# A hybrid recurrent diffusion step on one core: a new order for the last gates, splits and sums of the mixing stage

## The chip, the core and the metric

The kernel runs on one core of a Trainium2 chip. A core has TensorE (PE, matrix products into PSUM), VectorE (DVE), ScalarE (ACT, functions through tables), GpSimd (POOL) and SyncE (SP, whose queue here issues most loads). Each engine runs its own instructions in the order in which the program issues them, and waits at semaphores for the others. The metric is the device time of one execution in microseconds (us); a kernel is run several times and the median is told.

## The reference, cut to what matters

One layer for 640 tokens (128 of a prompt, 512 of a sample; 1024 features). The part around the change:

```python
hn = _rmsnorm(x, g_pre_mix) * (1 + sc1) + sh1
xa, ga, xs = jnp.split(hn @ w_in, [D_LRU, 2 * D_LRU], axis=-1)
ua = _dwconv(xa, conv_w, conv_b)
# both directions d, per block of 64 channels:
r = sigmoid(ua @ w_r[d] + b_r[d]);  i = sigmoid(ua @ w_i[d] + b_i[d])
log_a = -LRU_C * r * softplus(-lam[d]);  a = exp(log_a)
b = sqrt(-expm1(2 * log_a)) * (i * ua)
h = linear_scan(a, b, h0[d])
ya = gelu(ga) * (h[0] + h[1])
ys = ...                      # the S5 branch, 512 features
gate_a, gate_b = jnp.split(sigmoid(hn @ w_gate + b_gate), 2, axis=-1)
m = (gate_a * (ya @ w_proj_lru) + gate_b * (ys @ w_proj_s5)) @ w_out
x = x + g1 * _rmsnorm(m, g_post_mix)
# then a SwiGLU feed-forward (w_ff_in, w_ff_out), also normed and modulated
```

## The kernel before, in words

**Tiling.** Features lie on the 128 partitions, the 640 tokens along the free dimension, so 1024 features are eight tiles ("channels tiles" 0 to 7) of 128 x 640. Every fp32 product is made of three products of reduced-precision halves: high x high, low x high and high x low (`mtile`, lines 175 to 185), each in two halves of 320 tokens. So each weight block and each activation is *split* once: ScalarE copies it to its high part (`wh`, `yah`, `mh`), and VectorE subtracts that to get the low part (`wl`, `yal`, `ml`).

**Weights.** All weight blocks ("units") are listed in the order of use (lines 198 to 245). `split_next` (line 133) takes the next one: it allocates `wh` and `wl` from pools of three buffers each, issues ScalarE's copy and VectorE's subtraction, and then lets SP's queue issue loads up to four units ahead (`fetch_to`, four `raw` buffers). So a split waits for a load, for a free `wh` (which the products of the third unit before it must release), and its low part stands in VectorE's queue at the place where `split_next` was called. `use` splits on demand. Some units (blocks of `w_mod`) are not split: `mod_step` (line 569) multiplies them as they are, eight matmuls of one modulation step, into a PSUM tile that is held from the first step to the last.

**Tiles.** PSUM holds four tiles of 128 x 1024 fp32 (`psq`, line 67); one product takes one of them until its result is evacuated. Token tiles come from a pool of 20 (`ttile`), those of the recurrent unit from a pool of 27 (`lru`, line 1274). A new tile waits until a buffer is free; ScalarE, VectorE or GpSimd stand still meanwhile.

**The order is written out by hand** (`manual_schedule`, line 48): each engine's queue is the order of the calls. Around the change (lines 1307 to 1476):

- The loop at line 1307 runs over pairs of channel tiles of the recurrent unit; in its last round it makes the inputs of tiles 6 and 7. Then follows the tail of that unit for tiles 4 to 7, interleaved with the S5 projection.
- `gate_job(15)` (line 845): product of the sixteenth gate (`gate_mm`), its bias and two sigmoids on ScalarE, and a store to DRAM issued from ScalarE's queue. `gate_load` and line 1395 load gates back on GpSimd's queue (tiles `gld`, `gts`).
- `lru_gates(c)` (line 1172): four products of six matmuls (`q_gl`: two directions, r and i), each with a sigmoid on ScalarE (`ri`).
- `lru_scan(c)` (line 1220): four scans on VectorE into two tiles `hh` and their sum; `lru_mul(c)`: times the GELU branch; `lru_split(c)`: the two halves `yah`, `yal`; `lru_iu(c)`: i times u, two products on VectorE.
- `lru_decay` (line 1192): for two tiles, four tanh into tiles `ta`, then four exponentials in place, then whatever is passed as `then`, then four square roots; with table loads on ScalarE between. `lru_drive` (line 1212): for each tile four VectorE instructions, each 128 x 644.
- `ps5(m)` (line 1363), m = 0 to 7: an S5 projection of 24 matmuls (`q_p`), evacuated by a product with a gate on VectorE (`gld`). The sum over both branches is later made in the same tile.
- `pl_first(m)`, m = 0 to 2 (line 1378): the "first low part" of the output projection, over the first six of eight channel tiles, 36 matmuls (`q_pl`), copied to `plp` by ScalarE.
- The loop at line 1442 goes over the items `a0 a1 a2 f3 b0 f4 f5 f6 f7` (line 227). Items a are the low parts above, items f are whole projections of 48 matmuls; item b makes the "second parts" for m = 0 to 2 (12 matmuls each), adds them to `plp` and multiplies with the gate on VectorE. `mix_add(m)` adds the S5 part on GpSimd, `mix_split(m)` makes the halves `mh`, `ml`. Each item but the first begins with a `split_next` and, up to the eighth, a modulation step.
- `wo_mm(i, mid)` (line 1507): a block of 128 tokens times `w_out` (`q_wo`), 48 matmuls of 512 columns. `wo_evac` and `hn2_tile` norm the result and transpose it for the feed-forward.

All small arithmetic goes through helpers, so rows carry their lines: L59 is `tt` (VectorE or GpSimd, two tensors), L62 is `act` (ScalarE), L65 is `mm`, L130 a weight load on SP's queue, L1217 and L1229 the drive and the scans.

Of the kernel before, what the change touches and what calls it, by code (L numbers as in the profile page):

```python
# [39 lines left out]
def hybrid_step_kernel(ctx: ExitStack, tc: tile.TileContext, A, y_prompt, y_sample, o_lru, o_re, o_im):  # L40
# [92 lines left out]
    def split_next(eng=None, lo_eng=None, late=None):  # L133

        while state["split"] < len(units):
            i = state["split"]
            u = units[i]
            state["split"] += 1
            if not u["split"]:
                continue  # L140
            fetch_to(i + 1)
            pool, bufs = u.get("pool", (wp, 3))
            u["hi"] = pool.tile(u["shape"], F32R, tag="wh", bufs=bufs, name="wh")
            u["lo"] = pool.tile(u["shape"], F32R, tag="wl", bufs=bufs, name="wl")
            if eng is None:
                act(u["hi"], u["raw"], AF.Copy)
            else:
                eng.tensor_copy(out=u["hi"], in_=u["raw"])
            if late is None:
                tt(u["lo"], u["raw"], u["hi"], ALU.subtract, lo_eng)  # L150
            else:
                late.append(lambda: tt(u["lo"], u["raw"], u["hi"], ALU.subtract))
            fetch_to(i + 5)
            return True
        return False
# [689 lines left out]
    def gate_job(m, pool=None, q=None):  # L845
        q = gate_mm(m) if q is None else q
        g = ttile("gate", pool=pool)
        seg_act(g, q, AF.Sigmoid, shift(q, vec("b_gate", GO[m])))
        if pool is None:
            ACT.dma_start(out=gd[GO[m]], in_=g[:, 0:T])  # L850
        return g[:, 0:T]
# [320 lines left out]
    def lru_gates(c):  # L1172
        u, uh, ul, wh, wl = fr[c]
        r = {}
        for d, i in DI:
            q = psq("q_gl")
            a = 2 * d + i
            for b, (ww, xx) in enumerate(((wh, uh), (wl, uh), (wh, ul))):
                for h in range(2):
                    mm(q[:, 190 + 322 * h:190 + 322 * (h + 1)], ww[:, a], xx[:, 322 * h:322 * (h + 1)],  # L1180
                       b == 0, b == 2)
            t = ttile("ri", pool=lp)[:, 0:644]
            act(t, q[:, 190:834], AF.Sigmoid, bias=vec(("lru_b_r", "lru_b_i")[i], d * 8 + c))
            r[d, i] = t
        bk[c] = r
# [166 lines left out]
        warm(AF.Sigmoid)  # L1352

    gate_t = {}
    gate_job(15)

    def gate_load(m):
        gate_t[m] = ttile("gld")[:, 0:T]
# [4 lines left out]
    def ps5(m):  # L1363
        q = psq("q_p5")
        mtile(q, wblocks(U_PS[m // 2], 4, (m % 2) * 128, ahead=0), ys, range(4))
        t = gate_t.pop(8 + m)
        tt(t, q[:, 192:832], t, ALU.mult)
        mp.append(t)
# [9 lines left out]
    def pl_first(m):  # L1378
        q = psq("q_pl")
        pl_mm(q, "a", m, range(KP))  # L1380
        act(plp[:, m], q[:, 192:832], AF.Copy)

    split_next()
    lru_gates(6)
    lru_gates(7)
    for m in range(8, 14):
        gate_load(m)
    lru_scan(4)
# [4 lines left out]
    gts = htile("gts", F32, KD * T).rearrange("p (m t) -> p m t", m=8)  # L1393
    for m in range(8):
        POOL.dma_start(out=gts[:, m], in_=gd[m])
    split_next()
    ps5(0)
    lru_iu(6)
    lru_iu(7)
    gate_load(14)  # L1400
    gate_load(15)
    ps5(1)
    ta = lru_decay((6, 7), None, lambda: [lru_split(4), lru_split(5)])
    ps5(2)
    split_next()
    ps5(3)
    lru_drive(ta, (6, 7))
    for c in (6, 7):
        act(gel[c], gel[c], AF.Gelu_apprx_tanh)
    ps5(4)  # L1410
    split_next()
    ps5(5)
    lru_scan(6)
    split_next()
    ps5(6)
    lru_scan(7)
    ps5(7)
    lru_mul(6)
    lru_mul(7)
    split_next()  # L1420
# [20 lines left out]
    pt = {}  # L1441
    for j, (part, m) in enumerate(items):
        if j:
            split_next()
            if j < 8:
                mod_step(2, j, mod_raw(2, j))
            if part == "a":
                pl_first(m)
            elif part == "b":
                for i in range(NP1):  # L1450
                    q = psq("q_pl")
                    pl_mm(q, "b", i, range(KP, KD))
                    tt(plp[:, i], q[:, 192:832], plp[:, i], ALU.add)
                    tt(plp[:, i], plp[:, i], gts[:, i], ALU.mult)
                    pt[i] = plp[:, i]
                    mix_add(i)
            else:
                q = psq("q_pl")
                pl_mm(q, "f", m, range(KD))
                pt[m] = gts[:, m] if m < 7 else ttile("t7")[:, 0:T]  # L1460
                tt(pt[m], q[:, 192:832], gts[:, m], ALU.mult)
                if m < 7:
                    mix_add(m)
                for i in {NP1 + 1: (NP1,), NP1 + 2: (0, 1), NP1 + 3: (2, 4), NP1 + 4: (5,)}.get(m, ()):
                    mix_split(i)
        if j == 2:
            q = psq("q_nl")
            transpose(q[0:16, 0:128], nl.rearrange("p d k -> p (d k)"))
            nlo = ttile("nlo", pool=lp)
            DVE.tensor_copy(out=nlo[0:16, 0:128], in_=q[0:16, 0:128])  # L1470
            SP.dma_start(out=o_lru[0, 0].rearrange("d (k p) -> (d k) p", p=128), in_=nlo[0:16, 0:128])
        if j == 3:
            pre2 = mod_pre(2)
    mix_split(6)
    fetch_to(state["split"] + 4)
    lpool.__exit__(None, None, None)

# [378 lines left out]
```

## Time and profile before

| | us |
|---|---|
| median of three runs | 1039.13 |
| the three runs | 1036.62, 1039.13, 1042.95 |
| the profiled execution | 1037.07 |
| its span, first to last instruction | 1035.3 |
| TensorE busy | 989.7 |
| VectorE, ScalarE, GpSimd busy | 668.3, 461.0, 197.2 |

The mean granted clock of TensorE over the span is 0.988 of full speed (1.00 is the level of 2.4 GHz, 0.50 that of 1.2 GHz). In a timeline each row is one instruction or a run of equal ones: start and length in us from the start of the span, engine and line, operation, output tile <- input tiles, shape, count; in brackets how long the engine stood idle just before it, and whose instruction released it. A wait for several things is put down to the one that came last. Neighbouring rows overlap a little where instructions are pipelined.

### The profile page before, as it was taken

What the parts mean: (1) busy time and instruction counts of PE and PEld (TensorE: products, weight loads), DVE (VectorE), ACT (ScalarE), POOL (GpSimd) and SP (SyncE); (2) the same over time, 40 slices, a digit from 0 to 9 for tenths busy, and PEclk for the clock granted to TensorE, in tenths of its full rate; (3) what the DMA queues carried; (4) which work ended last, traced back from release to release, by engine and by line L of the source; (5) the groups of instructions that cost most, each with busy time, mean ns of one, the idle gap of its engine ahead of it and who ended that gap; (6) DMA issues with size and microseconds to landing.
All of it is one profiled execution on the core that took longest, in us unless ns stands there. A gap on an engine that the chain in (4) does not pass through costs nothing.

```text
span 1035.3 us, 16728 instructions
## 1 busy us (share of the span) xinstructions
PE 989.7 (96%) x6649; PEld 911.1 (88%) x6649; DVE 668.3 (65%) x1103; ACT 461.0 (45%) x748; POOL 197.2 (19%) x200
## 2 busy tenths in 40 slices
PE   5999999979999999999999989999999999999997
PEld 3698988879999999987877889999999999888885
DVE  5789899962477989782575785555555565434113
ACT  5535423234349889732242443444454454333112
POOL 4000000000000000300310274555555551000002
PEclk9999999989999999999999999999999999999999
DMA  9944276543213221747562312223322223522202
GB/s 305 322 115 128 68 210 199 186 152 96 63 42 102 61 73 49 259 133 210 178 201 104 121 43 82 81 83 87 96 83 82 83 82 122 206 79 82 70 13 101
DMA packets 135901, 125.57 MB, mean 121 GB/s; under 512 B 17320, under 2 KB 115384, under 8 KB 135824
## 3 DMA queue, kind: packets, MB, share of 16 engines
q1 hardware_dynamic: 129888, 111.82, 35.1%
q10 hardware_dynamic: 4080, 7.31, 2.1%
q0 software_dynamic: 1856, 5.38, 1.5%
q8 instruction: 52, 0.85, 0.3%
q14 instruction: 25, 0.20, 0.1%
HBM read 111.63 MB, written 12.85 MB: 120 GB/s over the span
## 4 chain that ended last, share of the span: by engine, by line
PE 73%; DVE 15%; ACT 5%; DMA 3%; issue 2%; SPq 0%; POOL 0%; ACTq 0%; DVEq 0%
PE f L65 15%; PE ffX L65 13%; PE q_g L65 6%; PE ffY L65 6%; PE q_pl L65 6%; PE q_xa L65 4%; PE q_wo L65 3%; PE ffZ L65 3%; PE q_ga L65 3%; DVE wl L59 2%; PE q_ff L65 2%; PE q_y L65 2%; PE q_m L65 2%; PE q_gl L65 2%; DVE F L59 2%
## 5 line engine op out<-in xcount | busy, mean ns | idle before, releaser
L59 DVE TENSOR_TENSOR wl<-raw,wh 128x1024 fp32r<-128x1024 f32 (+1 forms) x104 | 126.5, 1221 | 148.9 <-ACT wh L62 148.7
L62 ACT ACTIVATE wh<-raw 128x1024 fp32r<-128x1024 f32 (+1 forms) x106 | 110.5, 1047 | 180.2 <-PE f L65 81.9
L59 DVE TENSOR_TENSOR wl<-s,wh 128x1024 fp32r<-128x1024 f32 x38 | 55.1, 1450 | 60.8 <-ACT wh L62 60.8
L65 PE MATMUL f<-wl,ah 128*128 128x512 f32 x220 | 87.1, 396 | 0.0
L65 PE MATMUL f<-wh,ah 128*128 128x512 f32 x220 | 87.1, 396 | 0.0
L65 PE MATMUL f<-wh,al 128*128 128x512 f32 x220 | 87.1, 396 | 0.0
L65 PE MATMUL q_g<-hnh,wh 128*128 128x320 f32 (+1 forms) x256 | 60.8, 319 | 5.5 <-ACT Hst L62 5.5
L59 POOL TENSOR_TENSOR s<-raw 128x512 f32<-128x512 f32 x38 | 52.6, 1384 | 58.1 <-DVE wl L59 30.0
L65 PE MATMUL q_g<-hnl,wh 128*128 128x320 f32 (+1 forms) x256 | 59.4, 313 | 0.0
L65 PE MATMUL q_g<-hnh,wl 128*128 128x320 f32 (+1 forms) x256 | 59.3, 314 | 0.0
L65 PEld LDWEIGHTS f<-wl,ah 128*128 128x128 f32 x220 | 41.5, 188 | 9.9
L65 PEld LDWEIGHTS f<-wh,al 128*128 128x128 f32 x220 | 41.4, 188 | 10.0
L65 PEld LDWEIGHTS f<-wh,ah 128*128 128x128 f32 x220 | 41.4, 188 | 9.9
L65 PEld LDWEIGHTS q_g<-hnh,wh 128*128 128x128 f32 x256 | 43.5, 192 | 6.9 <-ACT Hst L62 5.7
L65 PE MATMUL ffX<-Th,wh 128*128 128x320 f32 x152 | 47.0, 310 | 0.0
L65 PE MATMUL ffX<-Tl,wh 128*128 128x320 f32 x152 | 47.0, 310 | 0.0
L65 PE MATMUL ffX<-Th,wl 128*128 128x320 f32 x152 | 47.0, 309 | 0.0
L62 ACT ACTIVATE u<-ffX 128x320 f32<-128x320 f32 x38 | 16.6, 438 | 64.3 <-PE ffX L65 64.3
L62 ACT ACTIVATE wh<-s 128x1024 fp32r<-128x1024 f32 x38 | 39.8, 1048 | 11.4 <-PE q_ff L65 6.0
L65 PEld LDWEIGHTS q_g<-hnl,wh 128*128 128x128 f32 x256 | 43.8, 192 | 0.0
L65 PEld LDWEIGHTS q_g<-hnh,wl 128*128 128x128 f32 x256 | 43.8, 191 | 0.0
L59 DVE TENSOR_TENSOR F<-F,sc 128x64 f32<-128x64 f32 (+1 forms) x128 | 39.5, 308 | 3.8
(388 smaller groups left out, 2803.9 us busy)
## 6 DMA issues: line engine op xcount, KB each, us to landing
raw<-in_w_ff_in SPq DMA_DIRECT2D x44, 512.0 KB
raw<-in_w_mod SPq DMA_DIRECT2D x32, 512.0 KB
raw<-in_w_ff_out SPq DMA_DIRECT2D x22, 512.0 KB
raw<-in_w_in SPq DMA_DIRECT2D x20, 512.0 KB
raw<-in_w_gate SPq DMA_DIRECT2D x16, 512.0 KB
wm<-in_w_mod SPq DMA_DIRECT2D x12, 512.0 KB
gd<-gate ACTq DMA_DIRECT2D x16, 320.0 KB
raw<-in_w_out SPq DMA_DIRECT2D x8, 512.0 KB
```

Of the source, the lines that this page charges most:

```text
L59: (eng or DVE).tensor_tensor(out=out, in0=a, in1=b, op=op)
L62: ACT.activation(out=out, in_=in_, func=func, **kw)
L65: PE.matmul(out, lhsT=lhsT, rhs=rhs, start=start, stop=stop, skip_group_check=True)
```

## The change

The product of gate 15 is still issued at its old place, but its bias, sigmoids and store come behind the four gates of tile 6. The split ahead of the gates of tile 6 goes behind those of tile 7. The split ahead of S5 projection 0 goes into `lru_decay`, between the exponentials and the square roots. `lru_drive` for tiles 6 and 7 is cut in two calls: tile 6 ahead of S5 projection 3, tile 7 behind the split and the GELUs that follow projection 3. Two more splits go behind S5 projections 5 and 7, where they stood behind 4 and ahead of 6, and the scans 6 and 7 follow them. In the item loop, item b no longer begins with a split: it comes behind the first of the three second parts. The mix splits are made one item earlier for the most part, and the last of them, of tile 6, inside the loop instead of behind it.

```diff
--- before.py
+++ after.py
@@ -1352,7 +1352,7 @@
         warm(AF.Sigmoid)
 
     gate_t = {}
-    gate_job(15)
+    gq15 = gate_mm(15)
 
     def gate_load(m):
         gate_t[m] = ttile("gld")[:, 0:T]
@@ -1380,9 +1380,10 @@
         pl_mm(q, "a", m, range(KP))
         act(plp[:, m], q[:, 192:832], AF.Copy)
 
+    lru_gates(6)
+    gate_job(15, q=gq15)
+    lru_gates(7)
     split_next()
-    lru_gates(6)
-    lru_gates(7)
     for m in range(8, 14):
         gate_load(m)
     lru_scan(4)
@@ -1393,28 +1394,28 @@
     gts = htile("gts", F32, KD * T).rearrange("p (m t) -> p m t", m=8)
     for m in range(8):
         POOL.dma_start(out=gts[:, m], in_=gd[m])
-    split_next()
     ps5(0)
     lru_iu(6)
     lru_iu(7)
     gate_load(14)
     gate_load(15)
     ps5(1)
-    ta = lru_decay((6, 7), None, lambda: [lru_split(4), lru_split(5)])
+    ta = lru_decay((6, 7), None, lambda: [split_next(), lru_split(4), lru_split(5)])
     ps5(2)
+    lru_drive(ta, (6,))
+    ps5(3)
     split_next()
-    ps5(3)
-    lru_drive(ta, (6, 7))
     for c in (6, 7):
         act(gel[c], gel[c], AF.Gelu_apprx_tanh)
+    lru_drive(ta, (7,))
     ps5(4)
+    ps5(5)
     split_next()
-    ps5(5)
     lru_scan(6)
+    ps5(6)
+    ps5(7)
     split_next()
-    ps5(6)
     lru_scan(7)
-    ps5(7)
     lru_mul(6)
     lru_mul(7)
     split_next()
@@ -1441,7 +1442,8 @@
     pt = {}
     for j, (part, m) in enumerate(items):
         if j:
-            split_next()
+            if part != "b":
+                split_next()
             if j < 8:
                 mod_step(2, j, mod_raw(2, j))
             if part == "a":
@@ -1454,6 +1456,8 @@
                     tt(plp[:, i], plp[:, i], gts[:, i], ALU.mult)
                     pt[i] = plp[:, i]
                     mix_add(i)
+                    if i == 0:
+                        split_next()
             else:
                 q = psq("q_pl")
                 pl_mm(q, "f", m, range(KD))
@@ -1461,7 +1465,7 @@
                 tt(pt[m], q[:, 192:832], gts[:, m], ALU.mult)
                 if m < 7:
                     mix_add(m)
-                for i in {NP1 + 1: (NP1,), NP1 + 2: (0, 1), NP1 + 3: (2, 4), NP1 + 4: (5,)}.get(m, ()):
+                for i in {NP1 + 1: (NP1, 0), NP1 + 2: (1, 2), NP1 + 3: (4, 5), NP1 + 4: (6,)}.get(m, ()):
                     mix_split(i)
         if j == 2:
             q = psq("q_nl")
@@ -1471,7 +1475,6 @@
             SP.dma_start(out=o_lru[0, 0].rearrange("d (k p) -> (d k) p", p=128), in_=nlo[0:16, 0:128])
         if j == 3:
             pre2 = mod_pre(2)
-    mix_split(6)
     fetch_to(state["split"] + 4)
     lpool.__exit__(None, None, None)
```

## Rows read from the trace of the kernel before

**Rows 1.** The page of the kernel before, part 1: busy time of TensorE.
```profile
PE 989.7 (96%) x6649; PEld 911.1 (88%) x6649; DVE 668.3 (65%) x1103; ACT 461.0 (45%) x748; POOL 197.2 (19%) x200
```

**Rows 2.** Timeline of TensorE, 412 to 531 us: start, length, instruction, [idle before <-releaser].
```profile
414.38 0.57 PE L65 MATMUL q_gl<-uh,lwh 128*128 128x322 f32 x2 [1.60 <-ACT gate L62]
...
416.53 0.90 PE L65 MATMUL q_gl<-uh,lwh 128*128 128x322 f32 x2 [0.99 <-ACT ri L62]
...
421.52 0.46 PE L65 MATMUL q_p<-ysh,wh 128*128 128x320 f32 x2
...
451.61 1.07 PE L65 MATMUL q_m<-raw,cst 128*32 128x512 f32 x8 [1.76 <-DVE gld L59]
453.30 0.64 PE L65 MATMUL q_pl<-yah,wh 128*128 128x320 f32 x2 [0.63 <-DVE gld L59]
...
492.95 0.53 PE L65 MATMUL q_pl<-yah,wh 128*128 128x320 f32 x2 [3.21 <-DVE plp L59]
...
530.59 0.73 PE L65 MATMUL q_wo<-wl,mh 128*128 128x512 f32 x2 [1.74 <-DVE wl L59]
```

**Rows 3.** Table by stages: stretch, its length, busy time of each engine, PEclk, DMA share.
```profile
416.00:419.40 3.40, 2.87 (x11) 2.88 (x12) 2.56 (x3) 3.33 (x5) 1.17 (x3) 0.50 1.01 315
...
453.50:457.00 3.50, 3.50 (x15) 3.50 (x15) 3.50 (x7) 0.00 (x0) 0.00 (x0) 0.51 0.93 305
...
493.00:528.90 35.90, 35.85 (x230) 32.47 (x230) 21.86 (x20) 11.63 (x15) 13.03 (x7) 1.00 0.44 148
...
617.40:620.80 3.40, 3.40 (x14) 3.40 (x14) 3.40 (x6) 3.39 (x6) 0.00 (x0) 0.50 0.54 158
```

**Rows 4.** Timeline of ScalarE, 413 to 442 us.
```profile
413.38 0.94 ACT L62 ACTIVATE gate<-q_g,shift 128x128 f32<-128x128 f32 x2
...
415.69 3.64 ACT L62 ACTIVATE ri<-q_gl,V 128x644 f32<-128x644 f32 x5
...
428.48 1.06 ACT L62 ACTIVATE wh<-raw 128x1024 fp32r<-128x1024 f32 x1 [5.96 <-PE q_p L65]
429.44 2.99 ACT L62 ACTIVATE ta<-ri,sp 128x644 f32<-128x644 f32 x4
...
433.75 3.01 ACT L62 ACTIVATE ri<-ri,sp 128x644 f32<-128x644 f32 x4
...
439.32 2.64 ACT L62 ACTIVATE ta<-ta 128x644 f32<-128x644 f32 x4
```

**Rows 5.** Timeline of VectorE, 417 to 452 us.
```profile
417.30 1.26 DVE L1229 TENSOR_TENSOR_SCAN hh<-ri,h 128x512 f32<-128x512 f32 x1
421.42 0.42 DVE L1229 TENSOR_TENSOR_SCAN hh<-ri 128x128 f32<-128x128 f32 x1 [2.86 <-PE q_gl L65]
...
429.57 1.22 DVE L59 TENSOR_TENSOR wl<-raw,wh 128x1024 fp32r<-128x1024 f32 x1 [0.27 <-ACT wh L62]
...
437.41 1.56 DVE L59 TENSOR_TENSOR yal<-hh,yah 128x640 fp32r<-128x640 f32 x2 [2.19 <-ACT yah L62]
...
442.72 0.96 DVE L59 TENSOR_TENSOR wl<-raw,wh 128x768 fp32r<-128x768 f32 x1 [3.02 <-ACT wh L62]
...
450.74 0.81 DVE L59 TENSOR_TENSOR gld<-q_p,gld 128x640 f32<-128x640 f32 x1
```

**Rows 6.** Timeline of SyncE's queue, 417 to 453 us.
```profile
417.07 14.09 SPq L130 DMA_DIRECT2D raw<-in_w_mod  x2
...
452.45 0.80 SPq L130 DMA_DIRECT2D raw<-in_w_mod  x2
```

**Rows 7.** Timeline of VectorE at the second parts, 490 us.
```profile
490.85 1.22 DVE L59 TENSOR_TENSOR wl<-raw,wh 128x1024 fp32r<-128x1024 f32 x1 [4.71 <-ACT wh L62]
```

**Rows 8.** Timelines of VectorE and GpSimd at the mix splits, 498 to 529 us.
```profile
526.47 2.93 DVE L59 TENSOR_TENSOR ml<-gld,mh 128x640 fp32r<-128x640 f32 x2
...
498.40 1.57 POOL L59 TENSOR_TENSOR gld<-plp,gld 128x640 f32<-128x640 f32 x1 [0.76 <-DVE plp L59]
...
526.63 2.09 POOL L59 TENSOR_TENSOR gld<-t,gld 128x640 f32<-128x640 f32 x1 [4.97 <-DVE t L59]
```

## The prediction, made before the changed kernel was run

> **What bounds the kernel now.** The page comes first: TensorE is busy for 96% of the span [rows 1]. What can be won in a reordering is therefore only time in which TensorE stands still, or runs at the lower of its two clock levels. So the second view is TensorE's own timeline through the stretch that the diff touches (412 to 531 us), read for the waits in brackets [rows 2]. There are six: 1.60 and 0.99 us among the gate products, 1.76 and 0.63 before the first low part, 3.21 after the second parts, 1.74 in the first output block. The reader is to see the name behind each arrow: four of the six wait for VectorE, none for a load. The third view, the table by stages, shows the granted clock [rows 3]: 0.50 of full speed at 416.0 to 419.4 and 0.51 at 453.5 to 457.0, each just behind a pair of those waits, that is 1.2 GHz instead of 2.4; but 1.00 behind the single wait of 3.21. Half of 3.4 and of 3.5 us is what these two stretches cost: I take 1.4 in the first, where TensorE had only 2.87 us busy, and 1.6 in the second. Waits (9.93) and slow clock (3.0) together are 12.9 us; the question for each part is how much of them stays.
>
> **Part 1, the sixteenth gate's sigmoid behind the first four gates.** The products of gate 15 hold one of four PSUM tiles. Now ScalarE runs its two sigmoids first and then a split, and the fourth gate product waits for the former (1.60), the fifth for the sigmoid behind the latter (0.99). Behind the change ScalarE is free for the first gate at the place where the gate's bias stands now, just ahead of 413.38 [rows 4]; I write 413.1. A sigmoid of that shape takes 3.64 / 5 = 0.73, so the first PSUM tile is free at 413.9: the fourth product waits from 412.8 to 413.9, 1.15 instead of 1.60. Then ScalarE frees a tile each 0.73 while TensorE needs about 0.9 for a product of six matmuls, so the next three don't wait. The gate's own work comes at 413.1 + 4 x 0.73 = 416.0: 1.2 for bias and sigmoids, and 0.4 in which the queue stands at the trigger of its store; four more sigmoids end at 420.5. The eighth product needs the gate's tile at 417.6; it is free at 417.2, 0.4 of slack. The store leaves some 3 us later; its only reader, the load of that gate on GpSimd's queue, is itself issued behind loads that wait for slots, so I count nothing. One wait of 1.15 where the clock fell behind 1.60 and 0.99: I take it that the clock stays up. TensorE then starts the first S5 projection at 418.5 instead of 421.5: 1.0 + 0.45 + 1.4 = 2.9, rounded to 3.0.
>
> **Part 2, the splits.** The split that stood ahead of gates 6 now stands behind gates 7: ScalarE 420.5 to 421.5, and VectorE, in order, can't begin scan 4 until that split's low part is done. That is the price: VectorE idles where it now runs the split and the first half of scan 4 (to 418.6) ahead of its wait for a slot, which ends at 421.42 [rows 5]. The gain: the next split, on which ScalarE stands 5.96 us until S5 projection 1 has released its weights, goes behind the exponentials, so tanh starts some 5 us earlier [rows 4], and with it exponentials and square roots; two VectorE waits further down (2.19 for the halves of y, 3.02 for a split behind the square roots) have no cause left.
>
> VectorE's line: now from 421.42 to the end of the fifth S5 evacuation (450.74 + 0.81 = 451.55) pass 30.1 us, with waits of 0.27, 2.19 and 3.02, so 24.6 of work. Behind the change it starts at 421.5 with 1.2 for the low part and 1.6 for the first scan half: 421.5 + 27.4 = 448.9, without a pause if ScalarE keeps ahead. Does it? Tanh 3.0, table load and exponentials 4.3, split, two halves of y, table load and square roots (2.64): 421.5 + 3.0 + 4.3 + 1.0 + 1.4 + 1.3 + 2.6 = 435.1. Tanh's tiles must wait for slots that scan 4 frees, up to about 3.5: 438.6. Halving the drive asks for them at 440: slack 1.4 or more. The drive in halves puts its first half (3.2) ahead of S5 evacuation 3 instead of behind it; up to evacuation 4 the sum stays, and that alone is worth nothing beyond filling the time in which the square roots come.
>
> TensorE: eight S5 projections take (449.85 - 421.52) / 8 = 3.54 each. From 418.5, four end at 432.7; each of the next needs a tile that VectorE evacuates in the order above, at about 432.7, 436.5, 440 and 443.9, so waits of 0.1 to 0.3 each, 0.5 in all, and the last ends at 447.4. The modulation step then waits for 448.9: 1.5, where 1.76 stands now. The 0.63 behind it goes, because the split that stands between evacuations 4 and 5 is moved behind both. First low part: 448.9 + 1.0 = 449.9 instead of 453.30, 3.4 us earlier. With no second wait behind the modulation step I take the clock to stay up: 1.6 more. So **5.0** from parts 1 and 2.
>
> The loads that these splits issue on SP's queue go with them. The first two modulation blocks, issued at 417.07 and 14 us later [rows 6], follow the low parts of the two moved splits: about 422.7 and 438 in the new order, and are wanted at 448.9. A low product is 36 matmuls of the kind of which a projection has 24, 5.3 us; so the splits moved behind evacuations 5 and 7, whose low parts end near 450.7 and 457, are wanted at 456.2 and 462.5. The thinnest cover is that of the next modulation blocks: issued at 452.45 now [rows 6], near 450.7 then, wanted at 455.2, 4.5 us later. I count nothing for it, and up to 1 us in the range.
>
> **Part 3, the sums of the second parts.** Now VectorE stands idle for 4.71 us at the low part of a split whose high part comes late on ScalarE [rows 7], and the sums that would empty the three tiles stand behind it; TensorE waits 3.21. With the first sum and product ahead of that split, one tile is free before, so TensorE goes on: **3.2**. What is late next: the second tile, wanted after one whole projection and a modulation step, 7.2 + 1.0 us on, while its sum stands 1.2 + 0.8 behind the split. The split itself is no earlier on ScalarE (it needs a weight buffer of the second parts), and its weights are wanted two projections later. From below: nothing is gained if the first sum is itself held, which would need VectorE to be over 4 us late there, more than its idle time.
>
> **Part 4, mix splits one item earlier.** Between the last projection and the first output block, VectorE now makes two low parts, 2.93 us [rows 8], ahead of the weight split that TensorE waits 1.74 for. One is left. Taken alone a low part is 0.8, and the pair shows that the second waited: GpSimd's add beside it took 2.09 against 1.57 alone. If the two shared evenly, the whole second half of the pair would be won, 1.3 to 1.4; if the later one stands until the add ends, the weight split now stands in its place and just 0.7 is won. The start and length of the pair speak for the latter (the add ends at 528.72, the pair at 529.40), so I take **0.65**, bounds 0 and 1.4. The Trainium skill says this too ("SBUF — State Buffer", Who interferes with whom): of VectorE with two SBUF inputs and GpSimd reading SBUF, the later one fully blocks. By it the sum is the one I took, by even sharing it would be 0.7 us better; the rows agree with it.
>
> **Sum.** 5.0 + 3.2 + 0.65 = 8.9 against the profiled execution's 1037.07 (span 1035.3 and 1.8 around it): 1028.2. That execution is 2.06 under the median of the runs, 1039.13; I add half of this: **1029.2**. Everything behind the first output block (row loads on SP's queue, the waits and transposes behind them) hangs on the same chain and moves along.
>
> **Rivals.** (A) *The clock falls once more, or VectorE is later.* The wait of 1.5 at 447.4 follows four small ones. If it again brings 1.2 GHz, 1.6 us come back, and a VectorE line later by 1 us costs 1 us there: 8.9 - 2.6 = 6.3, 1031.8. For it: two such stretches came behind waits of 2.4 to 2.6 in all. Against: none came behind 3.21 and 1.74. (B) *Parts 1 and 2 give nothing*: tanh's tiles, or scan 4 behind the moved split, put VectorE 3.4 us later than I have it, and the slow stretch stays; only parts 3 and 4 remain, 3.85: 1034.3. It decides from a fifth evacuation that ends after 451.5. (C) *More than forecast*: if the shifted waits ahead of 617.4 no longer bring the slow stretch there [rows 3], 1.7 us go, and if part 4 comes to its upper bound, 0.7: 1026.8. (D) *Slower than before*: S5 projections 4 to 7 now start one by one as tiles come free. If these short waits in a row bring 1.2 GHz there, four projections need 14.2 us more, of which the waits of about 1.5 are absorbed: 1029.2 + 12.7 = 1041.9; it turns the change into a loss once about 10.4 us of full-speed work runs at half speed. Against it, the waits are a tenth of the work between them. The Trainium skill names such a thing ("TensorE: Matmul & The Clock Gate", A second HAM failure mode): a kernel cycling through PSUM banks let TensorE idle so often that the clock swung. No run here shows it: the rows show a fall only behind longer waits.
>
> **How the numbers follow.** Forecast 0.57 (its own range 1027 to 1031.5), A 0.17, B 0.10, C 0.12, D 0.04. The range 1025 to 1034.5 holds the forecast, A, C and half of B. A change of about 1% is what a measurement of this kernel can tell; 1% under the median is 1028.7. Two fifths of the forecast lie below it, and nearly all of C: 0.38 faster. Slower by over 1% would be 1049.5; no case reaches it: 0.03. The rest, 0.59, is within 1%.
>
> **What would show it.** Right: S5 projection 0 near 418.5; no granted clock under 1.00 between 412 and 530; first low part near 450; no wait behind the second parts; tanh before 426; a wait of about 1.1 in the first output block. Wrong: VectorE pausing between 422 and 449, a wait of over 2 before the modulation step, or a new arrow to a load there.

## The result: 1.2% faster, 12 us instead of the forecast 9

The changed kernel takes 1024.85 us (median of four runs, 1024.77 to 1026.92), the kernel before 1038.77 beside it (four runs, 1036.62 to 1042.95): 0.9882 of the time, 95% interval 0.986 to 0.9903. (The quotient of these two medians is 0.9866, inside that interval.) The median is 0.15 under the low end of the range; ten runs of the changed kernel, six of them from a later series, have a median of 1027.07 and a mean of 1026.56, inside it; the first four ran at a mean clock of 0.9955, the later six at 0.9932. The profiled executions differ by 12.3 us in span (1035.3 and 1023.0), where the forecast was 8.9.

The page of the changed kernel answers to [rows 1]: TensorE has 6.5 us less busy time for the same 6649 matmuls. Those are not fewer products but fewer that ran at 1.2 GHz; the mean granted clock is 0.996, before 0.988.

```profile
PE 983.2 (96%) x6649; PEld 904.7 (88%) x6649; DVE 669.1 (65%) x1103; ACT 461.2 (45%) x748; POOL 198.0 (19%) x200
```

TensorE's timeline answers to [rows 2]; here again the bracket is the idle time just before the row and whose work ended it. The whole execution lies 0.87 us later at the gates (TensorE's wait begins at 413.66; it began at 412.78), so 0.87 comes off for a comparison.

```profile
414.81 0.56 PE L65 MATMUL q_gl<-uh,lwh 128*128 128x322 f32 x2 [1.15 <-ACT ri L62]
...
419.38 0.45 PE L65 MATMUL q_p<-ysh,wh 128*128 128x320 f32 x2
...
449.33 1.07 PE L65 MATMUL q_m<-raw,cst 128*32 128x512 f32 x8 [1.02 <-DVE gld L59]
450.33 0.56 PE L65 MATMUL q_pl<-yah,wh 128*128 128x320 f32 x2
...
484.72 0.56 PE L65 MATMUL q_pl<-yah,wh 128*128 128x320 f32 x2
...
521.61 0.73 PE L65 MATMUL q_wo<-wl,mh 128*128 128x512 f32 x2 [1.03 <-DVE wl L59]
```

Six waits of 9.93 us have become three of 3.20. At 484.72 a whole projection follows the modulation step directly: that is the place of the old wait of 3.21.

The table by stages answers to [rows 3] (stretch, length, busy time of PE, PEld, DVE, ACT, POOL, granted clock, DMA share, GB/s).

```profile
416.00:419.40 3.40, 3.40 (x25) 3.40 (x24) 0.00 (x0) 2.91 (x7) 1.05 (x2) 1.00 0.78 245
418.50:448.00 29.50, 29.48 (x198) 28.92 (x198) 25.61 (x37) 21.37 (x27) 6.92 (x13) 1.00 0.64 221
448.00:521.00 73.00, 71.57 (x474) 61.87 (x472) 48.01 (x56) 21.14 (x26) 14.63 (x8) 1.00 0.61 198
545.00:553.00 8.00, 8.00 (x41) 6.59 (x40) 4.06 (x8) 2.00 (x6) 0.00 (x0) 1.00 0.38 131
609.00:616.00 7.00, 7.00 (x49) 7.00 (x49) 7.00 (x7) 3.37 (x7) 5.48 (x3) 1.00 0.44 126
```

The clock is 1.00 in all five. The first three are the stretch of the change. The other two lie where the kernel before had two more slow stretches (stretches at 1.2 GHz), at 617.4 [rows 3] and at 549.1:

```profile
549.10:552.50 3.40, 3.30 (x12) 3.01 (x13) 1.33 (x6) 0.00 (x0) 0.00 (x0) 0.51 0.38 145
```

Neither is in code that the diff touches, and the waits ahead of them are still there (1.92 us at 538.07, 2.14 at 603.64; before 2.15 and 2.09).

ScalarE's timeline answers to [rows 4] and VectorE's to [rows 5]:

```profile
413.98 2.84 ACT L62 ACTIVATE ri<-q_gl,V 128x644 f32<-128x644 f32 x4
417.01 0.95 ACT L62 ACTIVATE gate<-q_g,shift 128x128 f32<-128x128 f32 x2
418.41 2.86 ACT L62 ACTIVATE ri<-q_gl,V 128x644 f32<-128x644 f32 x4 [0.46 <-ACT gate L62]
...
425.03 0.84 ACT L62 ACTIVATE ta<-ri,sp 128x644 f32<-128x644 f32 x1 [2.80 <-DVE hh L1229]
426.52 2.28 ACT L62 ACTIVATE ta<-ri,sp 128x644 f32<-128x644 f32 x3 [0.66 <-DVE nl L1230]
...
436.63 2.64 ACT L62 ACTIVATE ta<-ta 128x644 f32<-128x644 f32 x4
```

```profile
422.26 1.23 DVE L59 TENSOR_TENSOR wl<-raw,wh 128x1024 fp32r<-128x1024 f32 x1 [6.72 <-ACT wh L62]
...
448.46 1.55 DVE L59 TENSOR_TENSOR gld<-q_p,gld 128x640 f32<-128x640 f32 x2
...
518.20 0.81 DVE L59 TENSOR_TENSOR ml<-gld,mh 128x640 fp32r<-128x640 f32 x1
518.93 4.89 DVE L59 TENSOR_TENSOR wl<-raw,wh 128x1024 fp32r<-128x1024 f32 x3
```

On ScalarE tanh (`ta<-ri,sp`) now starts at 425.03, the square roots (`ta<-ta`) at 436.63. On VectorE the idle time of 6.72 is the price of the moved split; from 422.26 on there is no pause until the fifth S5 evacuation ends, at 449.28 (the first of the pair at 448.46). The last two rows are what became of [rows 8]: one low part, then the weight split, and here its run of three takes 4.89, where the same three took 3.48 before. The time that the second low part lost beside GpSimd's add now falls on the weight split.

**Where the 12.3 us come from.** Waits up to the first output block: 9.93 - 3.20 = 6.7. The slow stretches at 416 and 453, counted as in the prediction: 1.4 + 1.6 = 3.0. Those at 549 and 617, half of 3.4 each: 3.4. Less the 0.87 by which the gates came later: 6.7 + 3.0 + 3.4 - 0.9 = 12.2. In this pair of executions the difference from the forecast is thus for the most part the later pair of slow stretches. How often each stretch comes in other executions is told below.

### The profile page after: what moved, and what is told of

Its sections match the earlier page's. It is cut to its first block, busy times and chain, and to the rows that moved or that the text cites. A ratio compares the mean times of both kernels' runs of the same rounds, so it can differ in the third digit from the quotient of the medians.

```text
span 1023.0 us, 16723 instructions
## 1 busy us (share of the span) xinstructions
PE 983.2 (96%) x6649; PEld 904.7 (88%) x6649; DVE 669.1 (65%) x1103; ACT 461.2 (45%) x748; POOL 198.0 (19%) x200
## 4 chain that ended last, share of the span: by engine, by line
PE 74%; DVE 15%; ACT 5%; DMA 3%; issue 2%; SPq 0%; ACTq 0%; DVEq 0%
PE f L65 15%; PE ffX L65 13%; PE q_g L65 7%; PE ffY L65 7%; PE q_pl L65 6%; PE q_xa L65 4%; PE q_wo L65 3%; PE ffZ L65 3%; PE q_ga L65 3%; DVE wl L59 2%; PE q_m L65 2%; PE q_y L65 2%; PE q_ff L65 2%; DVE F L59 2%; PE q_xs L65 1%
## 5 line engine op out<-in xcount | busy, mean ns | idle before, releaser
L62 ACT ACTIVATE wh<-s 128x1024 fp32r<-128x1024 f32 x38 | 39.8, 1048 | 11.4 <-PE q_ff L65 6.0
```

Source lines behind the costliest of these rows:

```text
L62: ACT.activation(out=out, in_=in_, func=func, **kw)
```

## The experiments

Twelve kernels, one of them the changed kernel again, each timed beside the kernel before, all ratios against it. They come from four series, in which the kernel before itself has means of 1036.8 to 1038.7 us; a difference between kernels of two series is therefore surer by the ratios than by the microseconds. Theory A in the expectations is the reading above: a removed wait is worth what its bracket says, and the rest of the gain is the clock. The other letters are rivals that the expectations put beside it.

### Each part alone

Four kernels, each the kernel before with one part of the change. Part 1 alone, `p1_gate`:

```diff
-    gate_job(15)
+    gq15 = gate_mm(15)
...
     lru_gates(6)
+    gate_job(15, q=gq15)
     lru_gates(7)
```

> Part 1 alone in the kernel before: the sixteenth gate's sigmoids and store behind the gates of tile 6, the split left where it was. Theory A (the parts are worth what the waits say): the waits of 1.60 and 0.99 us become one of about 2.1, because ScalarE makes the split's high part first; TensorE gains 0.5, and 1.4 more if the clock stays at 2.4 GHz behind it. The 5.96 us that ScalarE stands at the next split stay, so the first low part starts 0.5 to 2 us earlier than the 453.3 of the kernel before. Time 0.5 to 2 us less. Rival B (the sigmoid order is the main thing): 3 us or more less.

1036.63 (ten runs), 0.9983 [0.9964, 1.0002]. One wait of 2.09 stands where 1.60 and 0.99 stood, because the split that the fifth gate had waited for is still ahead on ScalarE; 1.2 GHz still follows it, and the wait before the modulation step is the old one, 1.76. From TensorE's timeline in this kernel:

```profile
415.76 0.57 PE L65 MATMUL q_gl<-uh,lwh 128*128 128x322 f32 x2 [2.09 <-ACT ri L62]
...
451.94 1.06 PE L65 MATMUL q_m<-raw,cst 128*32 128x512 f32 x8 [1.76 <-DVE gld L59]
453.62 0.54 PE L65 MATMUL q_pl<-yah,wh 128*128 128x320 f32 x2 [0.62 <-DVE gld L59]
```

The gates' wait begins at 415.76 - 2.09 = 413.67, so the first low part comes 39.95 us behind it.

Part 2 alone, `p2_splits`: the splits, the halved drive and the scans as in the diff, gate 15 at its old place.

> Part 2 alone: splits, drive in halves and scans in the new order, the sixteenth gate at its old place. Theory A: the wait of 1.60 at the gate stays, that of 0.99 goes; VectorE's line from the first moved low part on bounds, as in the changed kernel, so the first low part starts within 0.5 us of where it does there (some 3.4 us earlier than before), and the two stretches at 1.2 GHz at 416 and 453 go: about 5 us less up to the end of that part. Each of the later stretches at 1.2 GHz (549, 617) may stay or go, 1.7 us each. Time 4 to 8 us less. Rival B (the gate order is needed for it): under 3 us less.

1033.47 (eight runs), 0.9954 [0.9935, 0.9972].

```profile
416.17 0.56 PE L65 MATMUL q_gl<-uh,lwh 128*128 128x322 f32 x2 [1.59 <-ACT gate L62]
...
450.23 1.06 PE L65 MATMUL q_m<-raw,cst 128*32 128x512 f32 x8 [0.79 <-DVE gld L59]
451.23 0.56 PE L65 MATMUL q_pl<-yah,wh 128*128 128x320 f32 x2
```

The gates' wait begins at 416.17 - 1.59 = 414.58, so the first low part comes 36.65 us behind it. In the whole change it is 450.33 - 413.66 = 36.67, before 453.30 - 412.78 = 40.52. Part 2 alone gives all that parts 1 and 2 win together up to the first low part, 3.9 us; part 1 alone gives 0.6 (39.95), and beside part 2 it adds nothing.

Part 3 alone, `p3_sums`:

```diff
-            split_next()
+            if part != "b":
+                split_next()
...
                     mix_add(i)
+                    if i == 0:
+                        split_next()
```

> Part 3 alone: in item b the split behind the first of the three second parts. Theory A: the wait of 3.21 us at 489.7 goes whole, no other wait in the stretch changes: 3.2 us less in that stage, and up to 1.7 more for each later stretch at 1.2 GHz that the shift makes disappear. Time 3 to 6.5 us less. Rival C (the wait moves to the next item): a new wait of TensorE behind the first whole projection, 1 us or more, and under 2 us less.

1033.55 (ten runs), 0.9947 [0.9929, 0.9966]. The wait of 3.21 is gone and no new one stands in its place. That is 5.4 us by the medians (1038.91 before, in the same series), more than the wait.

Part 4 alone, `p4_mix`:

```diff
-{NP1 + 1: (NP1,), NP1 + 2: (0, 1), NP1 + 3: (2, 4), NP1 + 4: (5,)}
+{NP1 + 1: (NP1, 0), NP1 + 2: (1, 2), NP1 + 3: (4, 5), NP1 + 4: (6,)}
...
-    mix_split(6)
```

> Part 4 alone: mix splits one item earlier. Theory A (the later of the two instructions stands until GpSimd's add ends): the wait of 1.74 us in the first output block becomes about 1.1; 0.65 us less there. Rival D (both share evenly): it becomes 0.3 to 0.4, 1.3 to 1.4 us less. Either way a later stretch at 1.2 GHz may come or go, 1.7 us each.

1038.36 (ten runs), 0.9993 [0.9971, 1.0015]: too small for the clock's scatter. The timeline shows it: the wait in the first output block is 1.01 us instead of 1.74.

```profile
533.78 0.74 PE L65 MATMUL q_wo<-wl,mh 128*128 128x512 f32 x2 [1.01 <-DVE wl L59]
```

The four gains, 0.17 + 0.46 + 0.53 + 0.07 = 1.23%, add up to the whole change's 1.18%, though each of them is known to about 0.2% only.

### Is the rest the clock?

The changed kernel once more, without an edit, for its scatter:

> The changed kernel once more, for the spread of its runs. Theory A (the rest of the gain beyond the waits is TensorE's clock: in each run each wait of some 2 us may or may not be followed by 3.4 us at 1.2 GHz, and the changed kernel has only two such waits left): runs between 1024.7 and 1028.5, in steps of about 1.7, with the mean granted clock from 0.996 down to 0.992, a median of 1025 to 1026.5. Rival E (the change does away with the later slow stretches for good): nearly all runs at 1024.8 and 0.996.

1027.42 (six runs, 1025.09 to 1029.42), 0.9893 [0.9869, 0.9916]: the median is higher than either theory had it. Its table by stages shows what differs from the first profile:

```profile
538.00:542.00 4.00, 1.62 (x11) 1.09 (x10) 1.80 (x4) 1.36 (x3) 0.00 (x0) 1.00 0.60 199
542.00:546.00 4.00, 4.00 (x21) 3.32 (x20) 3.38 (x10) 1.45 (x3) 0.00 (x0) 1.00 0.16 65
604.00:608.50 4.50, 2.51 (x18) 2.24 (x17) 4.40 (x5) 3.05 (x4) 3.38 (x3) 1.00 0.05 13
608.50:612.00 3.50, 3.50 (x15) 3.50 (x14) 3.50 (x5) 3.50 (x7) 0.00 (x0) 0.51 0.47 137
```

No fall behind 2.4 us of waiting at 539, but one at 608.5 behind 1.99; the first profile had none behind 2.14 at the same place. The same program with the same waits gets a slow stretch in one execution and not in another.

The fourteen profiled executions (before, changed, and one of each experiment) show how far that goes. Each row is a place and the wait that stands there:

| place (time before) | TensorE's wait, us | profiles with it | 1.2 GHz behind it |
|---|---|---|---|
| gates (416) | 1.6 and 1.0, or one of 2.1 | 6 | 6 |
| gates (416) | one of 1.15 to 1.6 | 7 | 0 |
| first low part (453) | 1.8 and 0.6 | 5 | 2: before, `p4_mix` |
| second parts (493) | one of 2.7 to 3.2 | 4 | 3: all but before |
| first transposes (549) | one of 1.7 to 2.4 | 8 | 2: before, `p2_splits` |
| feed-forward (617) | one of 2.0 to 2.1 | 11 | 6: 3 of 5 in the old order, 3 of 6 in the new |

Two of the places come out otherwise than in the profile of before. In `p1_gate` the waits before the first low part are as before and the clock stays up behind them, while the wait at the second parts is followed by 1.2 GHz; so it is in `p2_splits` and `p4_mix`. TensorE's timeline and the table by stages in `p1_gate`, then the tables of `p2_splits` and `p4_mix`:

```profile
490.67 0.53 PE L65 MATMUL q_pl<-yah,wh 128*128 128x320 f32 x2 [2.74 <-DVE plp L59]
```

```profile
453.60:457.00 3.40, 3.38 (x23) 3.40 (x24) 3.40 (x7) 0.00 (x0) 0.00 (x0) 1.00 0.89 287
492.00:495.40 3.40, 3.40 (x15) 3.40 (x14) 3.33 (x4) 0.00 (x0) 2.58 (x2) 0.50 0.68 228
```

```profile
489.90:493.30 3.40, 3.40 (x15) 3.40 (x14) 3.33 (x4) 0.00 (x0) 2.64 (x2) 0.50 0.65 223
```

```profile
496.50:499.90 3.40, 3.40 (x15) 3.40 (x14) 3.33 (x4) 0.00 (x0) 2.64 (x2) 0.50 0.55 200
```

Over many runs the clock gives an account of its own. 56 runs of the kernel before, from the first three series of experiments, have a mean of 1038.07 us and a mean clock of 0.9881; ten of the changed kernel 1026.56 and 0.9941. The time at 1.2 GHz is twice the missing clock times the span: some 24.6 us and 12.1. The 12.5 less are worth at most half, 6.3 us, less where TensorE waited in that time anyway. With 6.7 of waits that makes at most 13.0, against 11.5 measured. Within the 56 runs the time falls by 0.78 us for each 0.001 of clock; at that price the difference is worth 4.7 us, and 6.7 + 4.7 = 11.4.

Two of the parts bear this out. By the means `p2_splits` is 4.9 us faster than the kernel before of its series: its waits are 2.6 shorter, and its clock (0.9896 against 0.9876) is worth at most 2.1. `p3_sums` is 5.1 faster: 3.2 of wait, and at most 1.8 of clock (0.9893). Not all scatter is the clock, though: around that line the 56 runs still scatter by 1.5 us, and one run of the changed kernel took 1027.52 at 0.996, where others took 1024.8.

The direct test takes no wait of the kernel before away, but lets TensorE work in it: transposes of the identity whose result nobody reads, into unused columns of a tile that is held anyway, or through the kernel's own `keep_busy`. `b_fill`, on the kernel before:

```diff
+    def fill_q(n):
+        for _ in range(n):
+            transpose(mq[2][:, 512:640], ident)
...
+            if j == 5:
+                fill_q(24)
...
-        mid = {7: lambda: hn2_tile(i - 1)} if i else {3: lambda: mix_split(7)}
+        mid = {7: lambda: [keep_busy(16) if i == 1 else None, hn2_tile(i - 1)]} if i else {3: lambda: [mix_split(7), fill_q(12)]}
...
+    keep_busy(16)
     ff_mm(0, (1,))
```

> The kernel before with extra transposes, whose result nobody reads, put into four of TensorE's waits (489.7, 528.9, 547.0 and 614.5 us); the waits themselves and everything else stay. Theory A: the instructions behind the waits start when they did, but no stretch at 1.2 GHz follows there; what stays is those at 416 and 453. The runs lose about two stretches on average: 3 to 4 us less than the kernel before, mean granted clock about 0.991 to 0.992. Rival F (the slow stretches cost nothing, since TensorE waits for others behind them anyway, and the gain is the waits alone): the same time as before, within 1 us.

1034.76 (ten runs, all but one between 1034.5 and 1035.9), 0.9969 [0.9952, 0.9986]; by the means 1034.52 against 1037.78, 3.3 us. The timeline shows the transposes and what is left of the wait of 3.21, the table the clock behind it and at the two later places:

```profile
491.83 2.84 PE L104 MATMUL q_m<-ident 128*128 128x128 f32 x24
495.12 0.54 PE L65 MATMUL q_pl<-yah,wh 128*128 128x320 f32 x2 [0.45 <-DVE plp L59]
```

```profile
494.00:499.00 5.00, 4.55 (x33) 4.34 (x31) 4.90 (x7) 0.00 (x0) 2.33 (x2) 1.00 0.84 275
549.00:555.00 6.00, 6.00 (x40) 5.34 (x39) 4.15 (x12) 1.29 (x3) 0.00 (x0) 1.00 0.46 149
615.00:622.00 7.00, 5.43 (x38) 5.40 (x38) 7.00 (x8) 6.53 (x10) 3.14 (x3) 1.00 0.26 75
```

No dependence is shortened here, and yet the kernel is 3.3 us faster. The mean clock rises from 0.9883 to 0.9911, which is worth at most 2.9 us, so that the gain is the clock's as far as its interval (1.5 to 5.0 us) tells. That the scatter of the time shrinks with it fits the same cause. In its profile the stretch at 453 is missing too, though nothing was put there: one profile alone would have credited the transposes with it.

### What sets the first low part

Two kernels undo one half each of the changed gate stage. `a_split_ahead`, the changed kernel with the first moved split back ahead of the gates of tile 6:

```diff
+    split_next()
     lru_gates(6)
     gate_job(15, q=gq15)
     lru_gates(7)
-    split_next()
```

> The changed kernel with the first moved split put back ahead of the gates of tile 6; the gate stays behind them. Theory A (VectorE's line from the moved split's low part on sets the first low part): the first wait grows from 1.15 to 2.1, but VectorE makes the low part and half of scan 4 while ScalarE is at the gates, so its line to the fifth S5 evacuation ends some 2 us earlier, the wait of 1.02 ahead of the modulation step goes, and TensorE's own work sets the first low part: it starts within 0.5 us of where it does now. Time the same within 1 us. Rival H (the split's place is what the part is worth): 1 us or more longer.

1027.53 (four runs), 0.9893 [0.9868, 0.9918], the same as the changed kernel. The first wait is 2.14, with 1.2 GHz behind it, and the wait before the modulation step is gone.

```profile
415.80 0.56 PE L65 MATMUL q_gl<-uh,lwh 128*128 128x322 f32 x2 [2.14 <-ACT ri L62]
```

```profile
417.20:420.70 3.50, 3.50 (x16) 3.50 (x15) 1.38 (x2) 3.01 (x6) 0.84 (x2) 0.51 1.03 278
```

The first low part comes at 451.12, from gates whose wait begins at 413.66 as in the changed kernel: 0.8 later (at most 0.5 was expected), though 1.0 more of wait and 1.7 of half speed lie ahead of it. Most of the rest is absorbed: the wait of 1.02 and the 0.6 us that the projections lost in short tile waits are gone, and TensorE's own work sets the point.

`a_gate_first`, the changed kernel with gate 15's sigmoids back at their old place:

```diff
-    gq15 = gate_mm(15)
+    gate_job(15)
...
     lru_gates(6)
-    gate_job(15, q=gq15)
     lru_gates(7)
```

> The changed kernel with the sixteenth gate's sigmoids back at their old place, ahead of the gates of tile 6 (no split between). Theory A (with the splits in their new places VectorE's line sets the first low part, and ScalarE reaches the end of the gates at the same time in either order, so part 1 adds nothing): the first wait is 1.6 instead of 1.15, the one before the modulation step about 0.8 instead of 1.0, the first low part starts within 0.3 us of the changed kernel's when counted from the end of TensorE's work ahead of the gates (36.7 us there); time within 1 us of the changed kernel's ten runs (mean 1026.6). Rival B (part 1 holds some of the gain): the first low part 1 us or more later, and 1.5 us or more longer.

1028.15 (six runs), 0.9898 [0.988, 0.9916].

```profile
415.18 0.56 PE L65 MATMUL q_gl<-uh,lwh 128*128 128x322 f32 x2 [1.60 <-ACT gate L62]
...
449.26 1.07 PE L65 MATMUL q_m<-raw,cst 128*32 128x512 f32 x8 [0.79 <-DVE gld L59]
450.25 0.56 PE L65 MATMUL q_pl<-yah,wh 128*128 128x320 f32 x2
...
541.77 0.48 PE L104 MATMUL q_x<-ident,xw 128*128 128x128 f32 x1 [3.85 <-DVE xw L1537]
```

First low part: 450.25 - (415.18 - 1.60) = 36.67 us behind the start of the gates' wait, to the hundredth that of the changed kernel. With part 2 there, part 1 moves nothing up to that point. The mean is 1.7 us above the changed kernel's ten runs, but this kernel ran on another chip than the other experiments; by the ratios it is 0.5 us (0.9898 against 0.9893), which shows no difference. In its profile the wait before the transposes is 3.85 instead of 1.92, with 1.2 GHz around it. Its four feed-forward loads held SP's queue for 5.58 us instead of 4.51, and the rows behind them were issued later (527.07 instead of 526.15). That this is the whole cause is not shown, and why those loads took longer stays open.

### What is left to win

The changed kernel still waits in the first output block, before the first transposes, and inside the feed-forward. `a_rows_early` issues the two gain rows and the first tokens' rows ahead of the first output block instead of behind it:

```diff
+    for s in range(2):
+        SP.dma_start(out=G1[s], in_=gsc[0, s:s + 1, :].to_broadcast([128, D]))
+    x_load(0)
+    x_load(1)
     for i in range(5):
...
```

> The changed kernel with the two gate rows and the first two rows of x loaded ahead of the first output block, so ahead of four weight loads in the queue. Theory A: the wait of 1.92 us ahead of the first transposes goes, and with it the chance of a slow stretch there: 1.9 us less, up to 2.7 on average. Rival G (the loads can't start sooner, since their buffers come free with the last projection, or the weight loads behind them come later by as much): no change, or a longer wait of 1.03 in the first output block.

1029.92 (six runs), 0.9921 [0.9897, 0.9944]: slower than the changed kernel. The wait before the transposes is gone, but the last block of `w_out` now stands behind those rows in SP's queue. It is issued at 520.20 and lands 8.7 us later; TensorE waits for its split, and 1.2 GHz follows. SP's queue, TensorE's timeline and the table by stages:

```profile
520.20 0.44 SPq L130 DMA_DIRECT2D raw<-in_w_out  x1
```

```profile
530.02 0.90 PE L65 MATMUL q_wo<-wh,mh 128*128 128x512 f32 x2 [3.26 <-ACT wh L62]
```

```profile
530.40:533.80 3.40, 3.40 (x12) 2.65 (x11) 1.11 (x3) 2.68 (x5) 0.00 (x0) 0.50 1.20 290
```

`a_rows_behind` puts the same loads behind that last weight block, but ahead of the feed-forward's:

```diff
-        mid = {7: lambda: hn2_tile(i - 1)} if i else {3: lambda: mix_split(7)}
+        mid = {7: lambda: hn2_tile(i - 1)} if i else {1: row_loads, 3: lambda: mix_split(7)}
...
```

> The changed kernel with the four row loads behind the last load of the output weights and ahead of the four feed-forward loads (ahead of both, the last output weights came 8.7 us after their issue and TensorE waited 3.26 us for them). Theory A: the wait ahead of the first transposes (1.9 to 2.4 us) goes, no new one comes in the first output block beyond 1.03; 1.9 us less than the changed kernel, up to 2.7 on average with the slow stretches that this wait brings: 1023.5 to 1024.5. Rival G (buffers of the output weights or the feed-forward loads then come late): a new wait on a load of 1 us or more, and no gain.

1024.33 (five runs), 0.9883 [0.9864, 0.9902]; its mean is 1024.61, 1.9 below the changed kernel's ten runs. The kernel before was faster in this series too (1036.8): by the ratios (0.9883 against 0.9882 and 0.9893) the difference is within 1 us and not shown by the times. The transposes start without a wait; only the one in the output block is left:

```profile
521.21 0.74 PE L65 MATMUL q_wo<-wl,mh 128*128 128x512 f32 x2 [1.02 <-DVE wl L59]
...
537.48 1.03 PE L104 MATMUL q_x<-ident,xw 128*128 128x128 f32 x8
```

Between the two places of the same four loads lie 5.5 us of mean time, 4 by the ratios.

`a_fill` puts unread transposes into the remaining waits of the changed kernel: 8 in the first output block, 16 before the transposes, 16 ahead of the second half of the first feed-forward product.

> The changed kernel with extra transposes, whose result nobody reads, put into the waits that it has left behind the first output block (8 at 520.6, 16 at 538, 16 ahead of the second half of the first feed-forward product, 604). Theory A (these waits are where its runs still lose time to the clock): nothing behind them starts sooner, no stretch at 1.2 GHz follows them, the runs lie close together near the fastest ones of the changed kernel, 1024.8 to 1025.5, granted clock 0.995 to 0.996, so 1 to 2 us less than its mean of 1026.5. Rival E (the later slow stretches had gone anyway): the same as the changed kernel within 0.5 us.

1026.7 (six runs), 0.9906 [0.9884, 0.9928], mean 1026.69: no gain, a miss. The mean clock, 0.9943, is that of the changed kernel's ten runs (0.9941). The third group stands ahead of the wait at 604 and not in it, and waits of 0.54 and 1.54 stay. That there is less to win where the clock holds oftener already is an argument, not shown.

`a_all` joins the row loads behind the last weights, the split ahead of the gates, 16 transposes in the tile of the third gate product, which cover the wait that this split brings, and the fills of `a_fill` in the output block and ahead of the feed-forward.

> Row loads behind the last output weights, the first moved split back ahead of the gates of tile 6, and extra transposes (results unread) in three waits: 16 behind the third gate product of tile 6, 8 in the first output block, 16 ahead of the second half of the first feed-forward product. Theory A: with the split ahead the wait before the modulation step is gone (1.0), and with the transposes the wait of 2.14 at the gates no longer brings the clock down; the first low part starts 0.8 us earlier than in the changed kernel, the wait ahead of the first transposes is gone (1.9), and few stretches at 1.2 GHz are left: 1021.5 to 1023.5, granted clock 0.995 or more. Rival: the transposes hold up the gate's evacuation or the products behind them, and the first low part is no earlier: 1023.5 or more.

1021.87 (four runs, 1021.46 to 1024.2), 0.9861 [0.984, 0.9883]. All four lie below all ten runs of the changed kernel, by 4.2 us in the mean and by some 3 by the ratios, whose intervals overlap: the fastest version of this study. What each of its pieces gives was not taken apart.

```profile
415.88 0.56 PE L65 MATMUL q_gl<-uh,lwh 128*128 128x322 f32 x2 [0.35 <-ACT ri L62]
...
448.72 1.07 PE L65 MATMUL q_m<-raw,cst 128*32 128x512 f32 x8
449.72 0.56 PE L65 MATMUL q_pl<-yah,wh 128*128 128x320 f32 x2
```

```profile
413.00:585.00 172.00, 171.44 (x1031) 151.38 (x1029) 121.47 (x184) 72.46 (x109) 33.37 (x29) 1.00 0.57 184
```

Over 172 us from the gates into the feed-forward TensorE stands still for 0.56 us, and the clock is 1.00 throughout.

## Why the prediction was right, and which term was too small

**Part 1.** Each step came as put: the first wait 1.15 (forecast 1.15), no wait at the next gates, S5 projection 0 at 419.38 - 0.87 = 418.51 (418.5), clock 1.00. But the 3.0 us by which the projections start earlier are part 1's only in small part, and don't reach the first low part. From the start of the gates' wait to S5 projection 0 pass 421.52 - 412.78 = 8.74 us before, 6.53 with part 2 alone (421.11 there) and 5.72 in the whole change: 2.2 come with the moved split, 0.8 with the moved sigmoids. Those 0.8 are waited out behind: the eight projections take 448.32 - 419.38 = 28.9 us instead of the 28.3 of `a_gate_first` (420.13 to 448.47), since they need tiles that VectorE has not emptied yet, and the modulation step waits 1.02 instead of 0.79. VectorE's line sets that point, as the prediction's part 2 has it.

**Part 2.** VectorE's line lasts 449.28 - 422.26 = 27.0 us (27.4), without a pause. Tanh's tiles wait 2.80 + 0.66 = 3.5 us (up to 3.5). The S5 projections end at 448.32 - 0.87 = 447.45 (447.4), with 0.6 of short tile waits (0.5). The wait before the modulation step is 1.02 (1.5) and the 0.63 is gone. The first low part stands at 450.33 - 0.87 = 449.46 on the scale of before (449.9). No load became late.

**Part 3.** The 3.2 went whole, and `p3_sums` shows it alone. What that kernel won beyond it, 1.9 us by the means, fits the clock of its runs (at most 1.8): the prediction put nothing on the clock here, because the profile of before has 1.00 behind this wait, but in three of the four profiles where the wait stands 1.2 GHz follows it.

**Part 4.** 1.74 became 1.03, so 0.7 (0.65), and `p4_mix` gives 1.01 alone. Even sharing between VectorE and GpSimd would have left 0.3 to 0.4. The weight split, 1.4 us longer in the place of the pair's second low part, shows that whoever is later waits. That is what the Trainium skill states ("SBUF — State Buffer", Who interferes with whom), and the trace agrees.

**The term that failed** is the clock: "Waits (9.93) and slow clock (3.0) together are 12.9 us". It read slow stretches off one execution and gave each to its place. At the gates that holds in all six profiles with such waits; at 453 it holds in two of five, and behind the wait of 3.21, where nothing was put, 1.2 GHz comes in three of four. By these shares the three places are worth an estimated 1.7 x (1 + 0.4 + 0.75) = 3.7 us; that the 3.0 came so near is luck, since one stretch was counted too high and one left out. The stretches at 549 and 617 were taken as fixed, where rival C allowed for the later one alone; in the profiled pair both went, 3.4 us more. Over all runs the clock is worth 4.7 us by the slope over the 56 runs, at most 6.3, instead of 3.0. `b_fill` shows that work in the waits gives such time back. The sum of the waits was read nearly rightly: 6.2 put (9.93 less 1.15, 1.5 and 1.09), 6.7 measured.

**The chances.** It gave 0.59 to a change within 1% and 0.38 to a gain of more; the gain of 1.2% is the less likely of the two.

**The rivals.** A fell: no slow stretch came behind the modulation step, and its argument "none came behind 3.21" holds for that one execution only. VectorE was 0.5 us earlier than put, not later. B fell: the fifth evacuation ended at 449.28 - 0.87 = 448.41, not past 451.5. C came true in the profiled pair, for the stretch that it named and for the one at 549, but by chance rather than by the shift: behind the wait at 617 1.2 GHz comes about as often in the new order (3 of 6) as in the old (3 of 5). Part 4 stayed at the forecast value and not at the upper bound. D fell: from 418.5 to 448.0 the clock is 1.00, although the projections lose those 0.6 us in short tile waits. What the Trainium skill tells of waits of this kind ("TensorE: Matmul & The Clock Gate", A second HAM failure mode), that the clock swings with them, no run here shows.

## What to carry to other kernels

Where TensorE is busy for most of the span, a wait of about 2 us costs its own length and, in a part of the executions, half of a slow stretch behind it: count the second part over many runs and several profiles and over the whole kernel, not from one profile and the stretch of the edit. Reordering an engine that is ready early (here ScalarE's sigmoids) wins nothing at the point that another engine's line sets. In an in-order load queue such as SP's here, rows wanted soon go behind the last weights wanted sooner and ahead of the bulk of the next stage.

## What was unexpected of the hardware

The same wait was followed by 1.2 GHz in one execution and not in the next: 2.14 us at 603.6 without, 1.99 at 605.1 with, in the same program. A single wait of 3.21 left 1.00 in the profile of before, but 2.74, 3.00 and 3.19 at the same place in three other kernels did not, and 1.60 and 0.99 with a few matmuls between them never did (four profiles). Unread transposes in four waits made the kernel before 3.3 us faster without any dependence being shortened.
